# 76 float32r products on a zeroed tile ahead of the first modulation products

## The chip, the cores and the metric

The kernel runs on one core of a Trainium2 chip. The metric is the device time of one execution in microseconds (us); the median over several runs is compared. TensorE (PE) does the matrix products, VectorE (DVE), ScalarE (ACT) and GpSimd (POOL) the elementwise work, SyncE (SP) issues most of the transfers.

## The reference

One layer of a decoder trunk, for a prompt of 256 tokens and for 8 single-token samples with recurrent state, all in float32 with a model width of 2048. Cut to what matters here:

```python
mod = jax.nn.silu(c) @ p['w_ada'][l] + p['b_ada'][l]
sh1, sc1, gt1, sh2, sc2, gt2 = jnp.split(mod[:, None, :], 6, axis=-1)
h = rmsnorm(x, p['g_pre_mix'][l]) * (1.0 + sc1) + sh1
z = h @ p['w_in'][l]                      # 2048 x 15376
# three mixers of z: spatial gating, HGRN2, gated linear attention
merged = sum over n of gates[:, :, n] * (branches[n] @ p['w_branch'][l, n])
x = x + gt1 * rmsnorm(merged @ p['w_out'][l], p['g_post_mix'][l])
h2 = rmsnorm(x, p['g_pre_mlp'][l]) * (1.0 + sc2) + sh2
x = x + gt2 * rmsnorm(square(relu(h2 @ p['w_mlp_up'][l])) @ p['w_mlp_down'][l], ...)
```

The outputs are the new rows of prompt and samples, the recurrent states, and the normalised gating rows of the samples.

## The kernel before

Activations lie transposed, with the model width on the partitions: 16 blocks of 128 channels, each with 264 columns (256 prompt tokens and 8 samples). Every large product is made in three float32r parts, with both operands split into a high and a low part: high x high (line 602), high x low (line 603) and low x high (line 604), 264 columns each, summed in PSUM. ACT makes the high part of a weight block with a cast (line 109), DVE the low part with a subtraction (line 106), each on 128 x 512 elements.

`Stream` loads the weights in 512 KB pieces (lines 557 and 562) into four `raw` buffers (and two spare ones, `araw`), splits them two pieces ahead into six pairs of `whi` and `wlo`, and loads up to five ahead. `granule` issues the products of one piece. A load waits until the split of an earlier piece has freed its `raw` buffer; a split waits until products have freed a pair of `whi` and `wlo`.

Ahead of the first weight product, in this order on TensorE: transposes of the small inputs (lines 150, 151 and 251); the sum over partitions of the samples' squares (line 210, in `norm_rows`); the first half of the modulation products for four channel blocks' shift and scale (line 274, `First.steps`); eight transposes of the prompt's rows (line 241, `x_transposed`), which need the rows already scaled by the norm (`scale_rows`, lines 246 and 247); the rest of the modulation products around the transposes of the small vectors (lines 160 and 161); and the transpose of the modulation's sums (line 285). DVE and ACT then form the modulated activations (lines 414 and 416), split them, and the first product of line 602 can start.

`norm_rows` squares the prompt's rows on ACT (line 223) as they arrive, sums the samples' squares on DVE and TensorE, and makes both reciprocal roots in one short chain on DVE (lines 179 to 185), for prompt and samples together, in a tile of ten columns. So the scaling of the prompt's rows waits for the samples' sum of line 210 too.

The order on TensorE, SyncE and POOL is the written one in this part of the program (`manual_schedule`). The order on DVE and ACT is made by a planner, which places instructions by their written order and by when it reckons that they can start. Buffers are handed out from pools: `blk` gives one of 28 blocks of 128 x 1056 elements, `sm` one of three PSUM banks. POOL has, ahead of the place of the change, eight small transfers to issue (line 146) and the memset of `eps` (line 188).

Of the kernel before, what the change touches and what calls it, by code (L numbers as in the profile page):

```python
# [7 lines left out]
F32 = mybir.dt.float32  # L8
F32R = mybir.dt.float32r
# [6 lines left out]
P = 128  # L16
# [41 lines left out]
def hybrid_step_kernel(  # L58
# [8 lines left out]
    nc = tc.nc  # L67
    V, S, T = nc.vector, nc.scalar, nc.tensor
# [13 lines left out]
    def nm(s):  # L82
        uid[0] += 1
        return f"{s}_{uid[0]}"

    def blk(shape=None, dt=F32):
        shape = shape or [P, 4, NT]
        return blkp.tile(shape, dt, tag="b", name=nm("b"))

    def sm(shape=None):  # L90
        return psm.tile(shape or [P, 512], F32, tag="sm", name=nm("sm"))

    def tmp(shape, tag, bufs=2):
        return tp.tile(shape, F32, tag=tag, name=nm(tag), bufs=bufs)
# [155 lines left out]
    ps = sm([P, P])  # L250
    T.transpose(ps, xsr, ident)
    V.tensor_copy(xsT, ps.rearrange("p (b k) -> p k b", k=KT))
    xsn = tmp([P, KT, NS], "xsn", 1)
    rx = tmp([P, 2], "rx", 1)
    norm_rows(xt, xsT, xsn, rx)
# [1174 lines left out]
    for m in range(8):  # L1430
        if m in PRE_AT:
            n = N_PRE // len(PRE_AT)
# [289 lines left out]
```

## Time and profile before

| | |
|---|---|
| median of 3 runs | 1942.22 us (1941.23 to 1944.57) |
| profiled execution, span | 1942.9 us |
| TensorE busy | 1903.4 us (98%) |
| DVE, ACT, POOL busy | 1186.1, 1006.5, 83.9 us |
| mean granted TensorE clock | 0.994 |
| HBM traffic | 226 GB/s over the span |

The span is the time from the first to the last instruction of one profiled execution. PE busy is modelled from pipelined products, so 98% doesn't mean that TensorE runs at its peak; the granted clock (1.00 is full speed) stands beside each stretch of time in the tables by stretches. A row of the timeline has the start in us, the duration in us, the engine, the line of the program, the operation with its output and inputs, and in brackets the idle time before it with what ended that. SPq, ACTq and so on are the instruction queues that issue transfers. "PEld" is the load of the stationary operand.

### The profile page before, as it was taken

How to read it: one execution, taken by the hardware profiler on the slowest of the kernel's cores; microseconds unless marked ns; L12 is line 12 of the kernel's file. 1: busy time of each engine (PE TensorE's matmuls, PEld its weight loads, DVE VectorE, ACT ScalarE, POOL GpSimd, SP SyncE). 2: the span in 40 equal slices, each digit the busy share in tenths (PEclk: the TensorE clock that was granted, in tenths of full speed). 3: DMA queues.
4: the chain of work that ended last, by engine and by line, in shares of the span. 5: the costliest groups of instructions: out<-in, count | busy, mean ns of one | idle time of the engine just before them, and what ended most of it. 6: DMA issues, size and time to landing. Idle time of an engine off the chain costs nothing.

```text
span 1942.9 us, 42324 instructions
## 1 busy us (share of the span) xinstructions
PE 1903.4 (98%) x17080; PEld 1812.1 (93%) x17080; DVE 1186.1 (61%) x2103; ACT 1006.5 (52%) x1825; POOL 83.9 (4%) x142
## 2 busy tenths in 40 slices
PE   6999999998999999999999999999999999999998
PEld 5989999988999998999999988999999999999997
DVE  4566667686578695565555666545556555555665
ACT  5444454665666765544444556444444545454444
POOL 1000000001001112200000010000000000000000
PEclk9999999999999999999999999999999999999999
DMA  9897786688588688987777846776566555555552
GB/s 317 299 337 247 249 287 213 214 250 276 175 262 290 214 258 283 306 266 249 253 256 233 300 129 195 229 226 199 178 182 184 179 180 184 177 183 182 179 183 99
DMA packets 339380, 442.06 MB, mean 228 GB/s; under 512 B 14930, under 2 KB 281024, under 8 KB 339184
## 3 DMA queue, kind: packets, MB, share of 16 engines
q1 hardware_dynamic: 329120, 409.62, 65.5%
q0 software_dynamic: 8992, 28.48, 4.6%
q8 instruction: 134, 2.20, 0.5%
q10 hardware_dynamic: 1072, 1.25, 0.2%
q14 instruction: 62, 0.51, 0.1%
HBM read 427.60 MB, written 11.70 MB: 226 GB/s over the span
## 4 chain that ended last, share of the span: by engine, by line
PE 95%; DMA 2%; issue 1%; ACT 1%; DVE 1%; POOL 0%; SPq 0%; ACTq 0%; DVEq 0%; POOLq 0%
PE mm L602 29%; PE mm L603 29%; PE mm L604 28%; PE ada L342 3%; PE ada L274 1%; PE sm L633 1%; PE sm L780 1%; DMA raw<-in_w_in_dram 1%; PE sm L640 0%; DMA b<-in_x_prompt_dram 0%; DMA vbc<-vs_d 0%; DVE wlo L106 0%; DMA b<-in_w_ada_dram 0%; ACT gt L1515 0%; PE sm L1176 0%
## 5 line engine op out<-in xcount | busy, mean ns | idle before, releaser
L602 PE MATMUL mm<-b,whi 128*128 128x264 f32 x4624 | 1326.6, 287 | 7.5 <-ACT b L109 3.5
L603 PE MATMUL mm<-b,whi 128*128 128x264 f32 x4624 | 1317.8, 285 | 0.8 <-DVE b L106 0.8
L604 PE MATMUL mm<-b,wlo 128*128 128x264 f32 x4624 | 1314.5, 284 | 1.4 <-issue 0.7
L106 DVE TENSOR_TENSOR wlo<-raw,whi 128x512 fp32r<-128x512 f32 x1136 | 775.5, 689 | 572.0 <-ACT whi L109 570.0
L109 ACT CAST whi<-raw 128x512 fp32r<-128x512 f32 x1136 | 695.4, 618 | 730.6 <-PE mm L603 654.5
L602 PEld LDWEIGHTS mm<-b,whi 128*128 128x128 f32 x4624 | 872.3, 189 | 49.1 <-issue 26.2
L604 PEld LDWEIGHTS mm<-b,wlo 128*128 128x128 f32 x4624 | 872.5, 189 | 2.2 <-DVE wlo L106 1.1
L603 PEld LDWEIGHTS mm<-b,whi 128*128 128x128 f32 x4624 | 872.2, 189 | 1.4 <-DVE b L106 1.3
L103 DVE TENSOR_TENSOR b<-b,mm 128x528 f32<-128x528 f32 (+1 forms) x137 | 95.7, 700 | 42.7 <-PE mm L604 42.7
L1057 DVE SCALAR_TENSOR_TENSOR st<-vbc,b,st 128x128 f32<-128x128 f32 (+1 forms) x96 | 34.1, 389 | 51.1 <-DMA vbc<-vs_d 44.2
L1055 ACT ACTIVATE st<-st,fs 128x128 f32<-128x128 f32 (+1 forms) x96 | 37.0, 430 | 53.0 <-DMA st<-in_state_hgrn_dram 27.0
L274 PE MATMUL ada<-b,cT 128*32 128x256 f32 (+1 forms) x640 | 35.7, 361 | 7.2 <-DMA b<-in_w_ada_dram 7.0
L342 PE MATMUL ada<-araw,cT 128*32 128x512 f32 x296 | 39.9, 601 | 0.0
L274 PEld LDWEIGHTS ada<-b,cT 128*32 128x32 f32 x640 | 18.2, 115 | 19.7 <-issue 6.4
L100 DVE TENSOR_TENSOR b<-b,b 128x512 f32<-128x512 f32 (+1 forms) x47 | 34.1, 740 | 1.4 <-ACT b L1165 0.9
L1058 POOL DMA_DIRECT2D out_dram<-st x32 | 23.5, 735 | 156.6 <-DVE st L1057 150.8
L342 PE MATMUL ada<-b,cT 128*32 128x512 f32 x216 | 26.2, 593 | 0.0
L106 DVE TENSOR_TENSOR b<-gt,b 128x528 fp32r<-128x528 f32 x32 | 22.7, 708 | 3.9 <-ACT whi L109 0.9
L106 DVE TENSOR_TENSOR b<-b 128x1024 f32<-128x1024 f32 (+1 forms) x24 | 24.3, 1016 | 0.0
L109 ACT CAST whi<-araw 128x512 fp32r<-128x512 f32 x20 | 12.4, 621 | 20.7 <-PE mm L603 19.0
L100 DVE TENSOR_TENSOR gt<-vt 128x528 f32<-128x528 f32 x32 | 22.4, 701 | 0.9 <-ACT vt L1581 0.9
L1587 ACT ACTIVATE b<-vt 128x528 fp32r<-128x528 f32 x32 | 20.7, 647 | 1.0
(339 smaller groups left out, 825.2 us busy)
## 6 DMA issues: line engine op xcount, KB each, us to landing
raw<-in_w_in_dram SPq DMA_DIRECT2D x232, 512.0 KB, 4.7
raw<-in_w_mlp_up_dram SPq DMA_DIRECT2D x128, 512.0 KB, 3.7
raw<-in_w_mlp_down_dram SPq DMA_DIRECT2D x128, 512.0 KB, 3.6
b<-in_w_ada_dram SPq DMA_DIRECT2D x102, 512.0 KB, 6.4
araw<-in_w_ada_dram SPq DMA_DIRECT2D x74, 512.0 KB, 6.0
raw<-in_w_branch_dram SPq DMA_DIRECT2D x48, 512.0 KB, 4.5
raw<-in_w_out_dram SPq DMA_DIRECT2D x32, 512.0 KB, 3.9
b<-in_w_ada_dram SPq DMA_DIRECT2D x32, 256.0 KB, 5.7
```

Source lines behind the costliest of these rows:

```text
L100: V.tensor_tensor(o, a, b, op=ALU.mult)
L103: V.tensor_tensor(o, a, b, op=ALU.add)
L106: V.tensor_tensor(o, a, b, op=ALU.subtract)
L109: S.copy(hi, src)
L274: T.matmul(acc[32 * j:32 * j + 32, 0:n], cT[:, k, :], w[:, n * j:n * j + n], start=k == 0, stop=k == KT - 1)
L342: T.matmul(self.acc[32 * j:32 * j + 32, :], cT[:, k, :], ws[j // 2][:, j % 2 * 512:j % 2 * 512 + 512], start=k == 0, stop=k == KT - 1)
L602: T.matmul(o, a, xh(k + j), start=first and j == 0, stop=False)
L603: T.matmul(o, a, xl(k + j), start=False, stop=False)
L604: T.matmul(o, b, xh(k + j), start=False, stop=last and j == n - 1)
L1055: S.activation(st[:, i, :], st[:, i, :], AF.Copy, scale=fs[:, h0 + i, b:b + 1])
L1057: V.scalar_tensor_tensor(st[:, i, :], v[:, i, :], k[:, h0 + i, NP + b:NP + b + 1], st[:, i, :], ALU.mult, ALU.add)
L1058: nc.gpsimd.dma_start(G.s_out(b, h0, nh), st)
```

## The change

Between the copy of the samples' transposed rows (line 252) and `norm_rows`, the kernel takes one block `zf` in float32r, sets it to zero on POOL, and issues 76 products from it on TensorE. Both operands are parts of `zf`: 128 (in the last group 112) columns as the stationary tile, and 128 to 512 columns as the moving one. The results go to two PSUM tiles that nobody reads. There are 12 products of 512 columns; 8 each of 264, 256, 288, 320, 512 and 128; 8 of 264 that alternate between the two PSUM tiles; and 8 of 264 with a stationary tile of 112 columns. Nothing else is edited.

```diff
     ps = sm([P, P])
     T.transpose(ps, xsr, ident)
     V.tensor_copy(xsT, ps.rearrange("p (b k) -> p k b", k=KT))
+    zf, zs2 = blk(dt=F32R), [sm(), sm()]
+    nc.gpsimd.memset(zf.bitcast(F32), 0.0)
+
+    def fill(n, width, m=P, two=False):
+        zv = zf.rearrange("p k t -> p (k t)")
+        for i in range(n):
+            o = zs2[i % 2 if two else 0]
+            T.matmul(o[0:m, 0:width], zv[:, 0:m], zv[:, 512:512 + width], start=True, stop=True)
+
+    fill(12, 512)
+    for width in (264, 256, 288, 320, 512, 128):
+        fill(8, width)
+    fill(8, 264, two=True)
+    fill(8, 264, m=112)
     xsn = tmp([P, KT, NS], "xsn", 1)
     rx = tmp([P, 2], "rx", 1)
     norm_rows(xt, xsT, xsn, rx)
```

## The prediction, on record before the result

> **What bounds the kernel now.** I read the page first (busy shares, then the chain that ended last), then the table by stretches for the start and for the one later stretch where TensorE is short of work, then the timeline of the first 45 us, and last the chain there piece by piece.
>
> ```profile
> span 1942.9 us, 42324 instructions
> PE 1903.4 (98%) x17080; PEld 1812.1 (93%) x17080; DVE 1186.1 (61%) x2103; ACT 1006.5 (52%) x1825; POOL 83.9 (4%) x142
> ...
> PE 95%; DMA 2%; issue 1%; ACT 1%; DVE 1%; POOL 0%; SPq 0%; ACTq 0%; DVEq 0%; POOLq 0%
> ```
>
> TensorE carries 95% of the chain. A delay of its first weight product (line 602) is therefore a delay of the end, unless some later place has slack in which TensorE waits for something that the delay doesn't move. The profiled execution's span, 1942.9 us, is 0.7 us above the median of the runs (1942.22) and inside their range (1941.23 to 1944.57). I forecast by adding the shift to the median. Differences under 0.2% (3.9 us) count as no change: the three runs alone spread over 3.3 us.
>
> The stretches (columns: time, busy us of each engine, granted TensorE clock, DMA share, GB/s):
>
> ```profile
> 10.00:20.00 10.00, 6.55 (x71) 3.15 (x72) 3.76 (x17) 4.69 (x7) 0.00 (x0) 1.00 1.00 334
> 25.50:26.00 0.50, 0.00 (x0) 0.00 (x0) 0.17 (x3) 0.29 (x2) 0.00 (x0) 1.00 1.07 416
> 26.00:26.50 0.50, 0.00 (x0) 0.00 (x0) 0.39 (x5) 0.21 (x1) 0.00 (x0) 0.50 1.04 408
> 28.00:31.00 3.00, 2.65 (x10) 2.35 (x11) 3.00 (x7) 3.00 (x7) 0.00 (x0) 0.50 0.21 68
> 28.10:32.70 4.60, 4.35 (x18) 4.05 (x19) 4.13 (x8) 3.54 (x8) 0.00 (x0) 0.50 0.44 135
> 32.50:33.00 0.50, 0.50 (x5) 0.50 (x5) 0.00 (x0) 0.00 (x0) 0.00 (x0) 0.67 0.92 348
> 100.00:115.00 15.00, 11.72 (x79) 11.12 (x79) 13.19 (x30) 7.62 (x13) 0.00 (x0) 0.89 0.94 333
> ```
>
> From 10 to 20 us the DMA engines are full and TensorE isn't: the start waits for the weights of the modulation. The clock falls to 0.50 at about 26.0 us and is back at about 32.83 us (a mean of 0.67 in the half microsecond from 32.5 means a half clock for 0.33 of it). So the first weight products, from 28.18 us on, run at half speed for 4.65 us.
>
> The timeline of the start (start, us, engine, line, operation; in brackets the idle time before it and its releaser):
>
> ```profile
> 0.87 0.95 POOL L936 MEMSET att<- 128x1024 f32 x1
> ...
> 5.76 0.60 PE L210 MATMUL sm<-sqs,cst 128*128 128x8 f32 x2 [1.60 <-DVE sqs L103]
> 5.95 0.12 POOL L188 MEMSET eps<- 128x1 f32 x1
> 6.39 0.17 DVE L179 TENSOR_SCALAR sx<-sm 128x8 f32<-128x8 f32 x1 [0.69 <-PE sm L210]
> ...
> 12.86 0.17 DVE L179 TENSOR_SCALAR sx<-ss 128x2 f32<-128x2 f32 x1
> ...
> 15.31 2.19 ACT L246 ACTIVATE b<-b,rx 128x1024 f32<-128x1024 f32 x2 [2.68 <-DVE rx L230]
> ...
> 18.50 1.97 PE L241 MATMUL sm<-cst,b 128*128 128x128 f32 x8
> 18.56 1.75 SPq L562 DMA_DIRECT2D raw<-in_w_in_dram  x3
> 20.40 1.93 PE L274 MATMUL ada<-b,cT 128*32 128x128 f32 x32
> ...
> 22.86 1.08 PE L274 MATMUL ada<-b,cT 128*32 128x128 f32 x32
> ...
> 24.33 0.33 PE L285 MATMUL sm<-cst,gt 128*128 128x128 f32 x1 [0.39 <-ACT gt L278]
> ...
> 27.21 0.60 ACT L109 CAST whi<-raw 128x512 fp32r<-128x512 f32 x1
> ...
> 28.18 0.59 PE L602 MATMUL mm<-b,whi 128*128 128x264 f32 x1 [3.52 <-ACT b L109]
> ```
>
> The two modulation steps of equal size show the clock: 1.93 us at 20.40, 1.08 us at 22.86. Line 210, the sum over partitions for the norm of the samples, now runs at 5.76 us, long before anyone needs it: the norm waits for the prompt's squares, whose part enters at 12.86 us.
>
> Pieces of the chain at both speeds (start, us, what; 14 products from 29.74 to 32.60, 22 from 34.18 to 36.75):
>
> ```profile
> 29.74 0.22 PE mm L602
> ...
> 32.60 0.22 PE mm L603
> ...
> 33.75 0.44 PE sm L241 x4
> 34.18 0.12 PE mm L602
> ...
> 36.75 0.12 PE mm L602
> ```
>
> That is 2.86/13 = 0.220 us a product of 264 columns at the half clock (0.83 ns a column), 2.57/21 = 0.1224 us at the full one (0.464 ns a column), and 0.11 us a 128-column transpose at the full one.
>
> **The change part by part.** Nothing is removed. Added are one tile of the block pool, one memset on POOL, and 76 products on TensorE between the transpose of line 251 and the product of line 210, since TensorE and POOL issue in written order in this block. No DMA, no SyncE instruction, no work on DVE or ACT is added.
>
> *The memset.* It stands behind the memset of `eps`, which ends at 6.07 us; 1056 elements at 0.95 us per 1024 are 0.98 us, so the fill begins at about 7.1 us. Nothing else is waiting on POOL.
>
> *The products.* Columns: 12 x 512 = 6144; 8 x (264 + 256 + 288 + 320 + 512 + 128) = 14144; twice 8 x 264 = 4224; together 24512. No row shows an unbroken float32r run from the start of the program, so I bound it: all at full speed 24512 x 0.464 ns = 11.4 us, all at half speed 24512 x 0.83 ns = 20.4 us. I take the run at 28.18 us as the nearest row: half speed for 4.65 us, which is 5580 columns, then 18930 columns at 0.464 ns = 8.8 us; together 13.4 us. Products of 128 columns appear in the trace only in f32; I take the 0.11 us of the transposes for each of the eight in place of 0.06, +0.4 us. Fill: 13.8 us, to 20.9 us. The bank alternation and the 112-column stationary tile I price as the plain 264-column product; 16 products at half that much again would be 1 us, inside the bounds.
>
> *What is queued behind.* Everything on TensorE: line 210, then the modulation products (line 274), then the transposes (line 241). The modulation products would now start at 20.9 us with their weights landed, so they run without waits beside what follows. Line 210 sets the path: 0.63 us from it to line 179 (5.76 to 6.39), 2.45 us from line 179 to the scaling of the rows (12.86 to 15.31), 1.1 us for the first of the two scalings on ACT (half of 2.19): the transposes can start at 20.9 + 0.63 + 2.45 + 1.1 = 25.1 us, against 18.50 now. From there to the first weight product it is 9.68 us now (18.50 to 28.18). With the clock up, the eight transposes take 0.88 in place of 1.97 us and the first 32 modulation products 1.08 in place of 1.93: 7.74 us. First weight product at 32.8 us, against 28.18: **+4.65 us**. With those steps still at half speed it would be +6.6.
>
> *The clock at the first weight product.* Now TensorE's last product before it (line 285) ends at 24.66 us and the clock drops at 26.0. The chain from line 285 to the first product (ACT's table load, DVE, ACT's casts) is not touched, so its 3.5 us of idle TensorE stay, and I take it that the clock is lost again: saving 0. The other end is a clock that stays up: the 18 products of the 28.10 to 32.70 row then take some 0.1 us less each, 1.8 us.
>
> The Trainium skill (TensorE: Matmul & The Clock Gate, Part 1: The HAM clock gate) says that the clock falls after at least one idle window of about 3.4 us and that the windows run free. By that rule alone an idle stretch of 3.5 us would only sometimes lose the clock; here it went 1.35 us after the last product, so the trace shows less patience than the rule. By the rule the sum would be 4.65 - 1.8 = +2.9 us.
>
> *Behind the first product.* The weights' casts and subtractions on ACT and DVE don't need TensorE until the split buffers are full. Two later waits of TensorE come from ACT:
>
> ```profile
> 36.30 1.35 ACT L109 CAST whi<-raw 128x512 fp32r<-128x512 f32 x2 [0.40 <-PE mm L603]
> ...
> 40.59 1.35 ACT L109 CAST whi<-raw 128x512 fp32r<-128x512 f32 x2 [1.93 <-PE mm L603]
> ```
> ```profile
> 38.21 0.39 PE L602 MATMUL mm<-b,whi 128*128 128x264 f32 x1 [0.65 <-ACT b L755]
> 42.49 0.39 PE L602 MATMUL mm<-b,whi 128*128 128x264 f32 x1 [0.65 <-ACT b L755]
> ```
>
> ACT's casts before them had themselves waited for TensorE, so they move with it; I credit nothing, at most 1.3 us. SyncE's loads wait for buffers that these casts free, so the transfers move too. Sum: +4.65 us, 1946.9 us, with +1.5 (both credits) and +6.6 us as its own ends.
>
> **The rivals.** *The shift is absorbed.* The DMA engines fall to a share of 0.21 from 28 to 31 us because the loads behind the first ones wait for raw buffers. If ACT and DVE split the first weights during the fill, those loads go out earlier against TensorE, and the later shortage shrinks:
>
> ```profile
> 89.64 10.26 DMA raw<-in_w_in_dram
> ```
> ```profile
> SPq L562 <- DVE wlo L106: 22.0, 11, 4.8
> ```
>
> There TensorE is idle for 15 - 11.72 = 3.3 us and loses 0.11 x 15 = 1.65 us to the clock. If the loads stay ahead by 3.3 us up to there, all 4.9 us go and the time is 1942.0, not slower; with the clock up at the first product as well, 1940.2. Against it: within the first 130 us SyncE's loads wait 22.0 us for the subtractions that free their buffers (second row), so a lead can't grow over the four raw buffers. It decides from a lead of about one 512 KB load.
>
> *The clock stays up, or half the waits go.* The mechanism of the forecast with the credits above: +1.5 to +3.8, about 1944.8. For it: the fill leaves a warmer array than now. Against it: the idle 3.5 us.
>
> *DVE and ACT get another order.* Their order is planned. If the plan puts the six casts of the first weights before the scaling of the rows, ACT is blocked on a transfer:
>
> ```profile
> DMA to landing us min/median/max: 3.5/6.8/7.9
> ```
>
> Loads issued at 18.56 us land at about 25.4; six casts of 0.6 us bring the scaling to 29.1, transposes at 30.2, first product at 37.9: +9.8, 1952 us. If DVE's six subtractions stand first too, 3 us more. For it: the plan has to fill the time that the 76 products take. Against it: at present it puts only one such cast ahead of the casts of the activations (27.21 us).
>
> *The zeroed products don't raise the clock.* Then the fill ends at 28.6 us (20.4 us and 1.1 for the narrow ones at 0.246), transposes at 32.8, first product at 42.5: +14, 1956 us. Against it: nothing in the rows separates zero from other data; TensorE is busy either way.
>
> **How the numbers follow.** Forecast 0.50 (of which 0.10 under 3.9 us), clock or credits 0.18 (no change), absorbed 0.14 (0.10 faster by over 0.2%, since it then tends to bring the credits with it, 0.04 no change), other order 0.12 (slower), clock never up 0.06 (slower). Slower 0.40 + 0.12 + 0.06 = 0.58, rounded to 0.59; same 0.10 + 0.18 + 0.04 = 0.32, rounded to 0.31; faster 0.10. The range runs from 1941.2 to 1953.5: it leaves out about half of the absorbed cases, the last rival and the worse half of the reordering. The forecast's own range is 1943.7 to 1948.8.
>
> **What would show it.** Right: 76 products from about 7.1 to 20.9 us, the first ones 0.43 us for 512 columns and after some 4.65 us 0.24; line 210 behind them; line 241 at about 25 us and idle TensorE just before it, ended by ACT; line 602 first at about 32.8 us with a clock of 0.50; afterwards every stretch as now but 4 to 5 us later. Wrong: line 210 running before the fill; a first line 602 under 31 us; casts of `whi` on ACT ahead of line 246; or less idle time of TensorE between 100 and 115 us.

## The result and the profile after

The changed kernel takes 1951.95 us (median of 3 runs, 1951.82 to 1953.87) against 1942.22 us before: a ratio of 1.0046, with a 95% interval of 1.003 to 1.0061. It is slower by 9.7 us by the medians. The profiled executions differ by less: the span is 1950.1 us against 1942.9. In the changed kernel 1.85 us lie around the span (1951.95 - 1950.1); with the same around the span of before, its profiled execution took about 1944.75 us, which is at the slow end of its three runs. In later comparisons 28 runs of the kernel before at a time had medians of 1943.2 to 1944.1 us, so the three runs were on the fast side, and 7 to 10 us is what can be said of the change.

First the page of the changed kernel (busy time, and the chain by engine):

```profile
span 1950.1 us, 42470 instructions
PE 1911.6 (98%) x17156; PEld 1822.0 (93%) x17156; DVE 1186.8 (61%) x2103; ACT 1006.7 (52%) x1825; POOL 84.8 (4%) x143
...
PE 95%; DMA 2%; DVE 1%; ACT 1%; issue 0%; SPq 0%; POOL 0%; ACTq 0%; DVEq 0%
```

The shares are those of before: an average over the program says nothing of a loss in its first 40 us. (Lines behind the change have numbers 14 higher: the weight products are lines 616 to 618, the modulation products line 288.) The timeline of TensorE at the start:

```profile
7.03 14.45 PE L260 MATMUL sm<-b 128*128 128x512 f32 x76 [2.83 <-POOL b L254]
21.33 0.29 PE L210 MATMUL sm<-sqs,cst 128*128 128x8 f32 x2
21.54 1.95 PE L288 MATMUL ada<-b,cT 128*32 128x128 f32 x64
29.56 1.97 PE L241 MATMUL sm<-cst,b 128*128 128x128 f32 x8 [6.07 <-ACT b L246]
31.46 1.92 PE L288 MATMUL ada<-b,cT 128*32 128x128 f32 x32
...
37.20 0.59 PE L616 MATMUL mm<-b,whi 128*128 128x264 f32 x1 [1.63 <-ACT b L109]
```

The fill runs from 7.03 to 21.3 us as forecast. But the transposes come at 29.56 us, not at 25.1, after 6.07 us in which TensorE waits for ACT's scaling of the prompt's rows (line 246). ACT in that time:

```profile
24.36 1.14 ACT L109 CAST whi<-raw 128x512 fp32r<-128x512 f32 x2 [11.87 <-DMA raw<-in_w_in_dram]
26.23 1.89 ACT L109 CAST whi<-raw 128x512 fp32r<-128x512 f32 x3 [0.73 <-DMA raw<-in_w_in_dram]
28.36 2.19 ACT L246 ACTIVATE b<-b,rx 128x1024 f32<-128x1024 f32 x2 [0.24 <-DVE rx L230]
```

Five casts of weights now stand ahead of the scaling, and ACT sits idle for 11.87 us until the first weight piece has landed at 24.36 us. Most of that idle time costs nothing, since the norm can't be ready before about 24 us; the cost is the 4 us from there to the scaling at 28.36 us. DVE, whose chain for the norm's root leads to the scaling, has the matching subtractions in the middle of that chain:

```profile
21.65 0.17 DVE L179 TENSOR_SCALAR sx<-sm 128x8 f32<-128x8 f32 x1 [8.70 <-PE sm L210]
...
22.88 0.17 DVE L184 SCALAR_TENSOR_TENSOR sa<-sa,sx 128x10 f32<-128x10 f32 x1
25.01 0.69 DVE L106 TENSOR_TENSOR wlo<-raw,whi 128x512 fp32r<-128x512 f32 x1 [1.96 <-ACT whi L109]
25.62 0.16 DVE L185 SCALAR_TENSOR_TENSOR rr<-sa,rr 128x10 f32<-128x10 f32 x1
25.70 0.68 DVE L106 TENSOR_TENSOR wlo<-raw,whi 128x512 fp32r<-128x512 f32 x1
...
28.16 0.16 DVE L230 COPY rx<-rr 128x2 f32<-128x2 f32 x1
```

The chain is at its eighth step at 22.88 us and then waits for the cast of a weight piece; it ends at 28.16 us instead of about 24. The likely reason, which the rows don't show, is that the planner reckoned with the chain's wait for the 76 products and put the splitting of the first weights into that time; in the trace the first weights land at 24.36 us, later than the products end.

The clock, by stretches of the changed kernel (columns as in the prediction):

```profile
23.50:29.50 6.00, 0.00 (x0) 0.00 (x0) 4.25 (x12) 4.03 (x7) 0.00 (x0) 0.74 1.05 395
36.00:36.50 0.50, 0.00 (x0) 0.00 (x0) 0.50 (x4) 0.32 (x1) 0.00 (x0) 1.00 1.02 371
36.50:37.00 0.50, 0.00 (x0) 0.00 (x0) 0.43 (x5) 0.50 (x2) 0.00 (x0) 0.65 1.10 387
37.20:43.00 5.80, 5.80 (x25) 5.62 (x26) 1.86 (x6) 3.26 (x7) 0.00 (x0) 0.50 0.85 292
```

TensorE is idle from 23.5 to 29.5 us and loses the clock, so the transposes take 1.97 us as before. The clock comes back, and is lost once more at about 36.65 us (a mean of 0.65 from 36.5 to 37.0), in the idle 1.63 us ahead of the first weight product; so the first 24 weight products run at half speed again.

Where the delay goes can be read from modulation products that both chains hold. Of before, then of after (start, us, what):

```profile
46.15 1.89 PE ada L274 x64
85.70 1.86 PE ada L274 x32
130.35 1.86 PE ada L274 x32
493.13 0.86 PE ada L342 x8
1335.70 1.85 PE ada L342 x16
```
```profile
55.72 1.88 PE ada L288 x64
95.31 1.86 PE ada L288 x32
138.78 1.86 PE ada L288 x32
498.19 0.86 PE ada L356 x8
1342.97 1.85 PE ada L356 x16
```

The shift is 9.0 us at the first weight product (37.20 against 28.18), 9.6 at 46 and 86 us, 8.4 behind the shortage of weights near 100 us, 5.1 at 493 us and 7.3 at 1336 us; from there the two run alike. These are two single executions, and part of the ups and downs is where each of them happened to lose the clock: behind the same wait of 2.02 us (at 107.32 us before, at 116.97 us after) the kernel before lost it for 3.4 us and the changed one didn't, which is worth 1.2 us here.

### The profile page after: what moved, and what is told of

It is laid out like the page before. It is cut to its first block, busy times and chain, and to the rows that moved or that the text cites. A ratio compares the mean times of both kernels' runs of the same rounds, so it can differ in the third digit from the quotient of the medians.

```text
span 1950.1 us, 42470 instructions
## 1 busy us (share of the span) xinstructions
PE 1911.6 (98%) x17156; PEld 1822.0 (93%) x17156; DVE 1186.8 (61%) x2103; ACT 1006.7 (52%) x1825; POOL 84.8 (4%) x143
## 4 chain that ended last, share of the span: by engine, by line
PE 95%; DMA 2%; DVE 1%; ACT 1%; issue 0%; SPq 0%; POOL 0%; ACTq 0%; DVEq 0%
PE mm L616 29%; PE mm L617 29%; PE mm L618 28%; PE ada L356 3%; PE ada L288 1%; DMA raw<-in_w_in_dram 1%; PE sm L647 1%; PE sm L794 1%; DMA st<-in_state_gla_dram 0%; PE sm L654 0%; DMA b<-in_x_prompt_dram 0%; DVE wlo L106 0%; DMA b<-in_w_ada_dram 0%; ACT whi L109 0%; PE sm L241 0%
## 5 line engine op out<-in xcount | busy, mean ns | idle before, releaser
L1072 POOL DMA_DIRECT2D out_dram<-st x32 | 23.5, 735 | 154.1 <-DVE st L1071 153.3
```

Source lines behind the costliest of these rows:

```text
L1072: nc.gpsimd.dma_start(G.s_out(b, h0, nh), st)
```

## The experiments

Theory A: about half of the delay is the planner's new order on DVE and ACT, the rest the fill on the path through line 210. Theory B: the products by themselves make it, whatever the order. Theories C and D came up later and are stated in the expectations of the last four kernels. Where nothing else is said, a kernel computes all that the reference asks for; only the order and the products on the zeroed tile differ.

**The tile and the memset without the fill.**

```diff
-    fill(12, 512)
-    for width in (264, 256, 288, 320, 512, 128):
-        fill(8, width)
-    fill(8, 264, two=True)
-    fill(8, 264, m=112)
+    fill(1, 128)
```

> The changed kernel with one product of 128 columns in place of the 76: the block, its memset on POOL and the two PSUM tiles stay. Both theories (the order of DVE and ACT; the fill on TensorE by itself) expect what the kernel before has: the first product of the high parts at 28.2 us, 1942 us within 2 us. A time above 1945 would say that the extra block or PSUM tiles cost something by themselves.

1943.92 us against 1944.13, ratio 0.9997 (0.9986 to 1.0007); the first weight product is at 28.00 us. The block, the PSUM tiles and the memset cost nothing.

**All 76 products, the order kept.**

```diff
     def scale_rows(x, r):
         for hf in range(2):
-            S.activation(x[0][hf], x[0][hf], AF.Copy, scale=r[:, 0:1])
-            V.tensor_scalar(x[1][hf], x[1][hf], r[:, 1:2], None, ALU.mult)
+            a = S.activation(x[0][hf], x[0][hf], AF.Copy, scale=r[:, 0:1])
+            v = V.tensor_scalar(x[1][hf], x[1][hf], r[:, 1:2], None, ALU.mult)
+        scaled[:] = [a.ins, v.ins]
...
-                split(raw, hi, lo)
+                if i < 3:
+                    with tc.issue_after(scaled[0]), tc.issue_after(scaled[1]):
+                        split(raw, hi, lo)
+                else:
+                    split(raw, hi, lo)
```

> The changed kernel with all 76 products, but the casts and subtractions of the first three weight pieces are queued behind the scaling of the prompt's rows on ACT and DVE. Theory A (the planner's new order, in which ACT and DVE wait for weight transfers ahead of the scaling, makes about half of the delay): the scaling starts about 2.5 us behind line 210, at 24.1 us, the transposes at about 25.3 us with the clock still up, the first weight product at 33 to 34 us in place of 37.2, and the end at 1945 to 1948 us. Theory B (the 76 products by themselves make all of it, the order doesn't matter): first product at about 37 us and 1951 to 1952 us.

1946.66 us against 1944.13, ratio 1.0011 (1.0002 to 1.002). TensorE and ACT at its start:

```profile
21.24 0.29 PE L210 MATMUL sm<-sqs,cst 128*128 128x8 f32 x2
...
24.02 2.19 ACT L246 ACTIVATE b<-b,rx 128x1024 f32<-128x1024 f32 x2 [11.62 <-DVE rx L230]
...
25.22 1.09 PE L241 MATMUL sm<-cst,b 128*128 128x128 f32 x8 [1.81 <-ACT b L246]
26.24 1.08 PE L291 MATMUL ada<-b,cT 128*32 128x128 f32 x32
...
32.51 0.39 PE L623 MATMUL mm<-b,whi 128*128 128x264 f32 x1 [2.69 <-ACT b L109]
```

Scaling at 24.02, transposes at 25.22 us with the clock up (1.09 in place of 1.97 us), first weight product at 32.51: the start comes out as the prediction's sum had it (25.1 and 32.8). The same 76 products now cost 2 to 2.5 us instead of 7 to 10. Theory A holds here and theory B falls: order makes the larger part.

**The order alone, no product added.**

```diff
+    stream[0].split(0)
+    stream[0].split(1)
+    with tc.issue_after(last_split[0]), tc.issue_after(last_split[1]):
-    scale_rows(xt, rx)
+        scale_rows(xt, rx)
```

(`last_split` holds the last cast and subtraction of `split`.)

> The kernel before, without any fill, with the casts and subtractions of the first two weight pieces queued ahead of the scaling of the prompt's rows on ACT and DVE. Theory A: ACT waits for the first piece to land at 24.4 us and for the second at 26.2 us, the scaling starts at 27.5 to 28.4 us, the transposes at about 29 us and the first weight product at 37 to 39 us, so nearly the whole loss without one added product: 1949 to 1952 us. Theory B: the order costs little, under 2 us, 1942 to 1944 us.

1951.49 us against 1944.13, ratio 1.0036 (1.0023 to 1.0048), without any fill:

```profile
24.21 2.38 ACT L109 CAST whi<-raw 128x512 fp32r<-128x512 f32 x4 [11.92 <-DMA raw<-in_w_in_dram]
26.50 2.19 ACT L249 ACTIVATE b<-b,rx 128x1024 f32<-128x1024 f32 x2
...
27.70 2.18 PE L244 MATMUL sm<-cst,b 128*128 128x128 f32 x8 [9.85 <-ACT b L249]
...
36.15 0.39 PE L605 MATMUL mm<-b,whi 128*128 128x264 f32 x1 [1.62 <-ACT b L109]
```

ACT waits for the same transfer and the first weight product comes at 36.15 us. Casts in front of the scaling are enough for most of the loss.

**The fill behind line 210.**

```diff
-    fill(12, 512)
...
     norm_rows(xt, xsT, xsn, rx)
+    fill(12, 512)
...
```

> All 76 products, moved behind the product of line 210, so that the norm's chain on DVE isn't held up. TensorE is taken until about 21.4 us; the first modulation products follow to 23.4, the transposes at 23.4 us with the clock up. Theory A: the scaling is done by 17.5 us, but four casts stand ahead of ACT's eviction of the transposes; first weight product at 31 to 33 us, end at 1944.5 to 1947.5 us. Theory B (each microsecond of fill on TensorE delays the end): as the changed kernel, 1951 to 1952 us.

1947.06 us against 1944.13, ratio 1.0018 (1.0007 to 1.0029); transposes at 23.21 us, first weight product at 32.56. Against the changed kernel the transposes come 6.35 us earlier, but the first weight product only 4.64: four casts stand between the scaling and ACT's copies out of PSUM, and TensorE waits 3.01 us at line 299 for the copy of the modulation's sums. So with this order too ACT waits for a transfer; with order and place both mended nothing was run.

**Fewer products.** The first 12 of 512 columns alone, and 44 in all (4 in place of 8 in the later groups).

```diff
     fill(12, 512)
-    for width in (264, 256, 288, 320, 512, 128):
-        fill(8, width)
-    fill(8, 264, two=True)
-    fill(8, 264, m=112)
```

> The changed kernel with the first 12 products of 512 columns only, which end at about 12.3 us. Line 210 then comes before the prompt's squares are summed (12.5 us), so the scaling stays at 15.3 to 15.5 us, and the planned order on DVE and ACT is that of the kernel before. Theory A: no loss; the steps from 18.5 us on run at the full clock, but wait for the last modulation weights, so the first weight product is at 27.0 to 28.3 us, and the clock is lost again ahead of it: 0 to 1.2 us faster than before. Theory B (each added product delays the end): about 5 us slower.

```diff
-        fill(8, width)
-    fill(8, 264, two=True)
-    fill(8, 264, m=112)
+        fill(4, width)
+    fill(4, 264, two=True)
+    fill(4, 264, m=112)
```

> The changed kernel with 4 in place of 8 products in each group behind the 12 of 512 columns: 44 products, which end at about 17 us. On ACT the scaling stays ahead of all casts, but two casts come ahead of the copy of the modulation's sums and two more behind it. Theory A: scaling at 19.8, transposes at about 21 us, then ACT waits for weight pieces that land at 24.4 and 26.2 us: first weight product at 30 to 31.5 us, 1 to 3 us slower than before. Theory B (loss in proportion to the fill's length): about 4 to 5 us slower.

With 12 products: 1947.52 us against 1943.30, ratio 1.0023 (1.0014 to 1.0032). With 44: 1948.65 us, ratio 1.0034 (1.0022 to 1.0046). Both start close to what theory A has: first weight product at 28.69 and 29.40 us, 0.5 and 1.2 us late. Yet both lose about 4 to 6 us, so theory A doesn't cover them. A list of TensorE's longer waits up to 1220 us showed one kind that the kernel with one added product doesn't have near 580 us: 2.00 us with 12 products, which the profile puts down to DVE, and 1.48 us with 44, for nothing that the profile shows ("issue"). The first of them:

```profile
583.24 0.39 PE L614 MATMUL mm<-b,wlo 128*128 128x264 f32 x1 [2.00 <-DVE b L100]
```

**A bridge to hold the clock.** 24 products of 264 columns behind line 285 in place of the fill; and the same with the 12 of 512 at the start.

```diff
     run(first.rows())
+    fill(24, 264)
```

> No fill at the start; 24 products of 264 columns on the zeroed tile stand behind line 285 instead, in the 3.5 us in which TensorE waits for the first activations. They end at about 27.7 us, ahead of the first weight product at 28.2 us, which they should not delay. If the idle time is what loses the clock, the first weight products run at 0.12 in place of 0.22 us and the end comes 1.5 to 2.2 us earlier than before (ratio about 0.999). If the clock falls anyway, or if ACT and DVE can't feed products at full speed there, no difference.

> Both: the 12 products of 512 columns at the start and the 24 of 264 behind line 285. The clock should stay up from about 12 us on. Expected: first weight product at 27.0 to 28.3 us at full speed, 2 to 3 us faster than before; if the start is held by the landing of the last modulation weights alone, the same as with the 24 products alone.

The bridge does what it should at the start. Clock of the kernel with the bridge alone, from 26 to 33 us:

```profile
26.00:28.00 2.00, 1.02 (x7) 0.61 (x5) 1.38 (x5) 2.00 (x6) 0.00 (x0) 1.00 0.85 324
28.00:33.00 5.00, 5.00 (x41) 4.96 (x42) 3.46 (x7) 4.40 (x9) 0.00 (x0) 1.00 0.61 168
```

The clock stays at 1.00 through the first products, where it was 0.50, and the modulation products at 46.15 us before start at 43.40. About 1.0 of these 2.75 us is another start of the same chain in this execution (scaling at 14.67 us instead of 15.31, first weight product at 27.16 instead of 28.18), the rest the clock. All the same, 1944.85 us against 1943.30, ratio 1.0009 (1.0000 to 1.0018); with the warm-up as well 1944.97 us, ratio 1.0010 (1.0001 to 1.0019). The lead is gone behind 576 us. Rows of TensorE's timeline, of the bridge alone and of both together:

```profile
581.74 0.28 PE L612 MATMUL mm<-b,whi 128*128 128x264 f32 x1 [1.89 <-issue]
```
```profile
578.71 0.30 PE L650 MATMUL sm<-st,b 128*32 128x128 f32 x2 [2.11 <-issue]
```

The wait isn't all that is lost there. Behind it the kernel with the bridge alone runs at half the clock for 3.4 us, where the kernel before has 1.00 (from 583.0 to 586.5 us); so does the kernel with 12 products, from 584.7 us. That is worth up to 1.7 us more in each:

```profile
582.90:586.30 3.40, 3.40 (x17) 3.40 (x17) 2.84 (x6) 2.41 (x6) 0.00 (x0) 0.50 0.99 311
```

The changed kernel has such a wait too, a burst later, and the kernel with the order kept one of 0.67 us there:

```profile
598.97 0.41 PE L654 MATMUL sm<-st,b 128*32 128x128 f32 x3 [1.35 <-issue]
```

All of these stand at, or at most 3 us behind, a burst in which TensorE issues some 126 tiny products (32 columns) in 1.3 us, such as this one of the kernel before:

```profile
579.69 1.29 PE L633 MATMUL sm<-b 128*32 128x32 f32 x126
```

And in each of these stretches the list of DMA queues has one transfer of instructions (count, MB, share). For the bridge alone, from 576 to 583 us, and for the whole of the kernel before:

```profile
q8 instruction: 1, 0.02, 0.8%
```
```profile
q8 instruction: 134, 2.20, 0.5%
```

These are 134 transfers for 2 x 17080 recorded products and loads of TensorE: 255 in each. The Trainium skill (Runtime: NRT & Kernel Launch, Instruction fetch mechanics) says that engines are refilled in blocks of 16 KiB, 256 instructions, and that crossing a block is mostly hidden; the size agrees (2.20 MB in 134 transfers is 16.4 KB each). That gave theory C.

**Padding.** Tiny products (16 columns on a 32-column stationary tile) behind line 210, where TensorE waits for weights anyway: 36, 76 and 128 of them.

```diff
     norm_rows(xt, xsT, xsn, rx)
+    fill(36, 16, m=32)      # 76 and 128 in the other two
```

> The kernel before with 36 products of 16 columns on a 32-column stationary tile, behind line 210, where TensorE waits for weights: as many added products as in the kernel with warm-up and bridge, at next to no time. Theory C (TensorE's instructions arrive in blocks of 256, the end of a block that falls into a burst of tiny products makes TensorE wait, and added products move the ends): the start as before (first weight product at 28.2 us), but a wait of 1 to 2 us for nothing that the profile shows near 577 us, with an instruction transfer beside it, and 1 to 2.5 us more at the end. Theory D (the waits there come from the weights or from chance): no such wait and no difference.

> The same with 76 tiny products, as many as the changed kernel adds. Theory C: the wait sits at the later burst, near 590 us, as in the changed kernel (1.35 us there, 0.67 us with the order kept): 0.5 to 1.5 us more than before. Theory D: no difference.

> The same with 128 tiny products, which are 256 instructions with their loads of the stationary tile. Theory C: the ends of the blocks fall on the same products as before, so there is no such wait between 560 and 610 us and the time is that of the kernel before within 1 us. Theory D: no difference either; a theory in which each added instruction costs would give more than with 36 and 76.

With 36: 1949.35 us against 1943.22, ratio 1.0030 (1.0018 to 1.0042). With 76: 1942.63 us, ratio 0.9999 (0.9990 to 1.0008). With 128: 1944.04 us, ratio 1.0005 (0.9994 to 1.0015). So the cost of an added product is not its time, nor does it grow with their number. The waits for nothing shown, with 36 and then with 128 products:

```profile
582.71 0.30 PE L650 MATMUL sm<-st,b 128*32 128x128 f32 x1 [1.86 <-issue]
```
```profile
429.88 0.39 PE L614 MATMUL mm<-b,wlo 128*128 128x264 f32 x1 [1.12 <-issue]
```

With 36 it is where theory C put it. With 128, a whole block, there is none near 580 us, and the one that it has is that of the kernel before:

```profile
428.86 0.39 PE L604 MATMUL mm<-b,wlo 128*128 128x264 f32 x1 [0.69 <-issue]
```

The case of 76 went against the expectation: no such wait at all, though the changed kernel, with as many, has 1.35 us.

The traces settle most of this when TensorE's products and loads are counted from the start. In the kernels with 12, 24, 44 and (two of them) 36 added products, 10859 or 10860 of them are recorded ahead of the instruction that ends the long wait, whichever instruction of the program that is; in the changed kernel and the one with the order kept it is 11371, which is 10859 + 2 x 256. The wait that the profile puts down to DVE is at the same count, so it is one of these. The wait near 429 us comes behind 7538 in the kernel before, and behind 7794, 256 more, with the 128 tiny products. And in all seven TensorE goes on 2.2 to 2.5 us after the transfer of instructions beside the wait began. The kernel with 76 tiny products reaches the count of 11371 at 592.88 us. There the transfer had begun at 590.65 us, early enough that only 0.35 us pass between that instruction and the one before it. So the position of the block's end decides where the wait can be, and in these traces the start of the transfer decides how long it is; what sets that start wasn't tried. The order on DVE and ACT is no rival here: in the kernels with 36, 76 and 128 tiny products every recorded operation of the two engines (semaphores aside) stands in the order of the kernel before.

These waits don't explain all of the times, though. The 36 products lose 6.1 us by the medians, of which the profiled execution shows 1.86 and 0.65 us as such waits and 0.9 us at the start; the profiled one, at 1946.70 us, is also faster than most of that kernel's runs (1945.8 to 1951.2). Their mean granted clock, 0.9953 against 0.9956 before, doesn't explain it either. The rest stays open.

**The bridge, filled up to a whole block.**

```diff
     norm_rows(xt, xsT, xsn, rx)
+    fill(104, 16, m=32)
...
     run(first.rows())
+    fill(24, 264)
```

> The 24 products of 264 columns behind line 285 and 104 tiny ones behind line 210, 128 in all. Theory C: the first weight products at full clock as with the 24 alone, without the 1.89 us wait near 580 us: 1.5 to 3 us faster than before, 2 to 3 us faster than with the 24 alone. Theory D: as with the 24 alone, 1 to 2 us slower than before.

1940.14 us against 1943.22, ratio 0.9987 (0.9978 to 0.9996): 3.1 us by the medians, and the only kernel here that is faster than the one before; against the bridge alone the ratio goes from 1.0009 to 0.9987. Its clock at the first products, and no wait marked "issue" of 0.4 us or more up to 1220 us:

```profile
26.00:28.00 2.00, 1.84 (x16) 1.63 (x14) 1.39 (x8) 1.69 (x6) 0.00 (x0) 1.00 1.03 392
28.00:33.00 5.00, 4.63 (x35) 4.39 (x36) 4.00 (x8) 4.40 (x10) 0.00 (x0) 1.00 0.57 174
```

How much of this is the blocks isn't shown. The planner also moved two additions of the modulation forward on DVE in this kernel. And the runs' granted clock is higher, 0.9975 in the mean against 0.9956 before and 0.9961 with the bridge alone. As an estimate from these, 0.0019 of 1940 us is 3.7 us of TensorE's time, as much as the whole gain. The profiled execution, the fastest of the eleven, doesn't lose the clock near 480 us, where the one before runs at half speed for 6.8 us.

## Why the prediction was right or wrong

The direction was right and the time lies in the range, but the forecast's size, 4.65 us, was about half to two thirds of what came, and what came is the rival that had a chance of 0.12. That the range holds the time is owed to that rival's part of it, not to the forecast's mechanism.

- *The memset and the fill*: right. Start at 7.03 us (forecast 7.1), end at 21.3 (20.9). The narrow, alternating and 112-column products hold no surprise that would show in the sum.
- *Line 210 sets the path*: right, and shown. With the order kept, the scaling starts 2.8 us behind line 210 (21.24 to 24.02; forecast 0.63 + 2.45) and the transposes at 25.22 us.
- *"2.45 us from line 179 to the scaling of the rows"*: this is the step that failed. It took 6.7 us (21.65 to 28.36), because I carried over a chain's duration from a profile in which DVE and ACT had another order. The rival named the right mechanism, six casts ahead of the scaling (five came). That its 1952 us is the measured time to the microsecond is partly luck: its first weight product was to come at 37.9 us (37.2 came), nothing was to change behind it, and the start from 1942.22 us was low. I gave it too small a chance because "at present it puts only one such cast ahead". That row says how the plan looks when nothing holds the norm back. The change made DVE wait 8.7 us for line 210, and the plan changed with it. The kernel with the order kept and the one with the order alone show it from both sides.
- *The transposes and the modulation products at the full clock*: wrong in the changed kernel (1.97 and 1.92 us), since the wait for ACT cost the clock; right where the order is kept (1.09 and 1.08). That the stretch up to the first weight product was nevertheless 7.64 us (forecast 7.74) is a coincidence: with these steps at half speed the sum has 9.68 us, and 1.9 us of the difference is idle time that went from ahead of the first weight product (next point).
- *The clock lost ahead of the first weight product*: right in the changed kernel (0.50 from 37.2 to 43.0), though not by the 3.5 us of idle TensorE that the prediction kept: 1.63 us were left. ACT's table load (24.29 us before, 37.47 us after) and the cast of a weight (27.21 us before) no longer stand in that gap. The clock went 1.1 us after the last product (line 299, which ends at 35.57 us, to about 36.65 us). The rule that the prediction takes from the Trainium skill (TensorE: Matmul & The Clock Gate, Part 1: The HAM clock gate), which spoke for +2.9 us, asks for a whole idle window of about 3.4 us; this trace doesn't agree with that. The bridge shows that the idle time is the cause: in all three kernels with it the clock stays up there.
- *Nothing credited behind the first product*: about right in its sign, off in size. 1.2 us are given back near 100 us, where the clock isn't lost as it was in the profiled execution before; since both have the same wait there, that is likely the luck of the two executions and not the change. With the order kept, the shift of 4.3 us at the first weight product was 2 to 2.5 us at the end, and where the rest went isn't shown beyond such differences of the clock. So even the forecast's own mechanism came out at about half of its 4.65 us. The waits at 38 and 42 us stayed at 0.65 us each, only later, as forecast.
- *A span set against the median of other runs*: I added the shift to 1942.22 us; the profiled execution was probably one of about 1944.75 us. This makes up to 2.5 us of the 9.7 by the medians.
- *What no part of the prediction had*: added instructions move the ends of the blocks in which TensorE's instructions arrive, and a wait of 1.35 us at 599 us came with it.

## What to carry to other kernels

Where a planner orders some engines, the cost of delaying one engine isn't the delay alone: ask what ready work the planner will put into the gap that it makes on the others, and on which transfer that work waits. Work that nobody needs is free only if nothing on the path is queued behind it, and it should stand where its engine waits for something that it can't delay. A difference of one or two microseconds after adding or removing instructions may come from where the instruction blocks end, or from where the clock happened to be lost. Pad by a whole block, and compare the granted clock of the runs, before giving it another cause.

## What the runs showed of the hardware that was not expected

- TensorE can wait for its own instructions. After bursts of some 126 products in 1.3 us it stood for 0.67 to 2.11 us, in seven kernels always at the same count of instructions or 2 x 256 further, and went on 2.2 to 2.5 us after an instruction transfer had begun; 36 added products brought such a wait near 580 us and 128 didn't. The Trainium skill (Runtime: NRT & Kernel Launch, Instruction fetch mechanics) calls the crossing of a block mostly hidden; behind these bursts it wasn't.
- In the profiled executions the stretches at half the clock that end inside the program last 3.41 us or two or three times that (from 26.00 to 32.83 us before, 36.65 to 43.48 us after), and where they fall differs from one execution to the next.
- The granted clock in the stretches reads 1.00 from the program's start, also where the products show half speed. The 12 products of 512 columns in the kernel with these alone took 4.98 us, 0.415 us each, in stretches marked 1.00:

```profile
7.03 4.98 PE L260 MATMUL sm<-b 128*128 128x512 f32 x12 [2.80 <-POOL b L254]
```

  At the full clock's 0.464 ns a column it would be 0.24 us. So at the start the duration of products, not the column of the clock, says which clock it is. Products on zeros did raise the clock: the modulation products behind the fill took 1.95 us for 64, against 1.93 us for 32 at half speed.
